# Norms of three groups summed over the partitions on GpSimd, row sums in fours, and equal last columns

## The chip, the cores and the metric

The kernel runs on one core of a Trainium2 chip. The metric is the time of one execution on the device, in microseconds. The engines are named as in the profile: PE is TensorE (PEld its weight loads), DVE is VectorE, ACT is ScalarE, POOL is GpSimd, and SP issues the DMAs.

## What is computed

Two layers of a decoder trunk over 1024 tokens of 1024 features, all in float32. In each layer one input projection feeds four mixers of 256 features each, called a, b, c and d; each group is normalized by itself, then all go through one output projection; a SwiGLU feed-forward block follows. Cut to what matters:

```python
for l in range(DEPTH):
    h = rmsnorm(x, attn_norm[l])
    proj = h @ w_in[l]
    y_a = mla_attention(...)        # latent attention, 4 heads, causal
    y_b = short_gated_conv(...)
    y_c = multiscale_pool(...)
    y_d = swa_sink_attention(...)   # window of 128 keys, a sink per head
    groups = jnp.stack([y_a, y_b, y_c, y_d], axis=2)
    gf = groups * lax.rsqrt(jnp.mean(groups * groups, axis=-1, keepdims=True) + RMS_EPS)
    x = x + (gf.reshape(b, s, D_MIX) * mix_norm[l]) @ w_o[l]
    h2 = rmsnorm(x, ffn_norm[l])
    gate, up = jnp.split(h2 @ w_gate_up[l], 2, axis=-1)
    x = x + (jax.nn.silu(gate) * up) @ w_down[l]
return rmsnorm(x, final_norm)
```

## The kernel before

Features lie on the 128 partitions and tokens along the free axis, so an activation of 128 features is a tile of 128 x 1024, kept as two halves `t` of 512 tokens. SBUF is managed as 47 slots (`u0` to `u46`) of two such halves. Every matrix product is made of three products of a rounded high part and a low part of each operand (`mm3`, L273), which `split` (L284, L285) makes with a cast on ACT and a subtraction on DVE.

*Norms.* `SumSq` squares tiles on ACT (L314, L319) and adds them on DVE (L324, L328), which leaves one tile of sums per partition. `rnorm` must then add over the partitions and give every partition the result: a product with a 128 x 128 matrix of ones on PE (L336) into a bank of PSUM. ACT takes logarithm, exponential and square (L338 to L340), DVE refines the root (L341, L344). `group_scale` does this for groups b, c and d in two halves, and multiplies the group by the result; `group_split` splits it for the output projection, whose products (`out_part`) read group d, then c, then b. Group a has its own `norm_a`.

*Window attention* (`swa_unit`). One unit is one block of 128 queries and one pair of heads: scores (L559) into PSUM, a masked minimum of negated scores (L569), two exponentials with row sums (L582), then on tiles of two columns the sink's term (L592, L593), its sum (L594), a reciprocal (L595), and the scaling (L597), transposes (L608) and products with the values (L620). Two units share the bank of the values, and what follows it.

*Latent attention* (`scores`, `mix_values`). For a head and a half, four blocks of 128 queries each get scores (L954 to L956), a maximum (L959, L962), exponentials with row sums (L973, L976), a sum of the two chunks' row sums where there are two (L985), a reciprocal (L986) and a scaling (L989, L992). `mix_values` transposes them (L1008), splits, and multiplies with the values (L1020). It works one step behind `scores`. In the last block POOL zeroes a part of the padded tile (L1017).

*Feed-forward.* The first of the 22 blocks of features is computed plainly for both halves, the others by a Strassen-like scheme (`gu_start` and after it, with L1234 copying a bank of PSUM to SBUF). For the plain block `plain_gates` multiplies the gate by the norm, `plain_silus` applies silu (L1368) and the norm again (L1369), and `plain_acts` multiplies by the other half of the block. The program calls them for the first half before the second half's norm, `norm(1)`, is taken. Silu belongs to another function table of ACT than logarithm and exponential.

*The end.* The last term of the last layer's down projection (`tail`, with `LAST_COLS`) is computed for four output tiles in two ranges of columns, so that the final norm and the output of the first range run beside the products of the second.

*Order.* The program is first written down in the order of the Python code. `order_engines` then arranges the instructions of each engine: `arrange` walks through a small model of the engines with a duration for each operation (`MM_NS`, `length`) and picks by rank, and the table `MOVED` shifts the rank of single steps. So the order on each engine comes from these numbers and not from the source alone.

Of the kernel before, what the change touches and what calls it, by code (L numbers as in the profile page):

```python
# [12 lines left out]
F32 = mybir.dt.float32  # L13
F32R = mybir.dt.float32r
AF = mybir.ActivationFunctionType
ALU = mybir.AluOpType
# [29 lines left out]
LAST_COLS = (slice(0, 384), slice(384, HT))  # L46
# [3 lines left out]
PC_N = 39  # L50
# [65 lines left out]
def trunk_kernel(ctx: ExitStack, tc: tile.TileContext, ins, out):  # L116
# [23 lines left out]
    nsink = cpool.tile([P, L * 4], F32, name="nsink")  # L140
# [158 lines left out]
    class SumSq:  # L299


        def __init__(self, n, direct=()):
            self.n, self.direct = n, direct
            self.acc = [None, None]
            self.done, self.rest = {}, {}
# [24 lines left out]
        def rnorm(self, t, cols=whole, tag="t"):  # L330

            a, n = F.ap(self.acc[t])[:, cols], self.n
            p = ps(tag)[:, cols]
            parts = [a] + [q for k, q in self.rest.items() if k == (t, cols.start)]
            for i, q in enumerate(parts):
                pe.matmul(p, ones, q, start=i == 0, stop=i == len(parts) - 1)  # L336
# [7 lines left out]
            dve.scalar_tensor_tensor(out=a, in0=q, scalar=1.5, in1=r0, op0=ALU.add, op1=ALU.mult)  # L344
            return self.acc[t]
# [83 lines left out]
    for l in range(L):  # L429
# [55 lines left out]
        if l == 0:  # L485
# [12 lines left out]
            for i in range(L):  # L498
                for o, c, n in ((nsink, PC_SINK, 4), (nffn, PC_FFN, NK)):
# [46 lines left out]
        psy_of = {}  # L546

        def swa_unit(g, i):
# [17 lines left out]
            nm, rs = small(2), small(2)  # L566
            for h in range(2):
# [6 lines left out]
                    scalar=nsink[:, l * 4 + 2 * g + h : l * 4 + 2 * g + h + 1],  # L574
# [4 lines left out]
            pr = tmp("tp")  # L579
            p3 = pr.rearrange("p (h k) -> p h k", h=2)  # L580
# [9 lines left out]
            es = small(2)  # L590
            sk = par[:, l * PC_N + PC_SINK + 2 * g : l * PC_N + PC_SINK + 2 * g + 2]
            dve.tensor_tensor(out=es, in0=nm, in1=sk, op=ALU.add)  # L592
            act.activation(es, es, AF.Exp)  # L593
            dve.tensor_tensor(out=rs, in0=rs, in1=es, op=ALU.add)  # L594
            dve.reciprocal(rs, rs)  # L595
# [16 lines left out]
            if i % 2 == 0:  # L612
                psy_of[g] = ps("pv")
            py = psy_of[g]
# [15 lines left out]
            if i % 2:  # L630
                pyv = py.rearrange("p (i h q) -> p i h q", i=2, h=2)
                tt = tmp("tn")
                tvs = [tt[rows, 0:256].rearrange("p (i q) -> p i q", i=2) for rows in (hd, tl)]
                for h, tv in enumerate(tvs):
                    act.copy(tv, pyv[tl, :, h, :])
                for h, (rows, tv) in enumerate(zip((hd, tl), tvs)):
                    o = F.ap(y["d"][g][t])[rows, (b - 1) * P : (b + 1) * P]
                    dve.tensor_tensor(
                        out=o.rearrange("p (i q) -> p i q", i=2),
                        in0=pyv[hd, :, h, :],  # L640
                        in1=tv,
                        op=ALU.add,
                    )

        units = deque((g, i) for g in range(2) for i in range(NK))

        def swa_some(n):
            for _ in range(n):
                if units and qs[2 * units[0][0]][1] is not None:
                    g, i = units.popleft()  # L650
                    swa_unit(g, i)
                    if i == NK - 1:
# [7 lines left out]
        def group_scale(g):  # L660

            sg = SumSq(2 * P)
# [267 lines left out]
        def scores(h, t, q):  # L930
# [3 lines left out]
            diag = ((own[0], 0), (own[1], 0), (own[0], P), (own[2], 0))  # L934
            for b in range(4):
# [9 lines left out]
                rs = small(2)  # L945
# [26 lines left out]
                if nch == 2:  # L972
                    act.activation(  # L973
                        chunks[0], pts[0], AF.Exp, bias=nm, scale=1.0, accum_out=rs[:, 1:2]
                    )
# [6 lines left out]
                    accum_out=rs[:, 0:1],  # L982
# [1467 lines left out]
```

## Time and profile before

| what | value |
|---|---|
| median of 3 runs | 2061.03 us (2056.88 to 2061.2) |
| profiled execution | 2059.23 us |
| its span, first to last instruction | 2057.4 us |
| granted clock of TensorE | 0.998 |
| PE busy | 2041.4 us (99%) |
| DVE busy | 1605.9 us (78%) |
| ACT busy | 988.1 us (48%) |
| POOL busy | 6.2 us |
| attention of layer 0, of layer 1 | about 103 to 390 us, 1045 to 1400 us |

Busy time is the union of an engine's instructions. Matmuls overlap in the pipeline, so what one costs is read from the start of one to the start of the next and not from its own duration (0.39 us for 512 columns). In a row of the groups of instructions stand line, engine, operation, tiles and shapes, count, then busy time, mean duration in ns, and the idle time before them with what ended it. In a row of the timeline stand start, duration, engine, line, operation and count, and in brackets the idle time before it. In a row of the waits stand who waited for whom, the sum in us, how often, and the longest.

### The profile page before, as it was taken

The numbers are of one execution on the slowest core, as the hardware profiler recorded it, in microseconds if no ns is written. First come the engines' busy times: TensorE is split into PE (matmuls) and PEld (weight loads), VectorE is DVE, ScalarE is ACT, GpSimd is POOL, SyncE is SP. The second block draws the span as 40 slices with busy tenths as digits, with TensorE's granted clock in tenths as the row PEclk, the third lists the DMA queues.
The fourth block names the chain that finished last, engine by engine and source line by source line (L and its number), as shares of the span: only waits on it lengthen the run. The fifth ranks groups of instructions, "written<-read, shape, count | busy, mean of one in ns | idle before, by whom it ended". The sixth has DMA issues, their size and how long they took to land.

```text
span 2057.4 us, 26139 instructions
## 1 busy us (share of the span) xinstructions
PE 2041.4 (99%) x9418; PEld 1681.8 (82%) x9418; DVE 1605.9 (78%) x2860; ACT 988.1 (48%) x1729; POOL 6.2 (0%) x36
## 2 busy tenths in 40 slices
PE   9999999999999999999999999999999999999998
PEld 7887888888888888888788878887888888888888
DVE  7889988999778778455576898989987877875555
ACT  6447666753333335344443666758433332354342
POOL 0000000000000000000000000000000000000000
PEclk9999999999999999999999999999999999999999
DMA  5020223255445448665401103142554544486642
GB/s 182 24 72 21 81 67 129 106 182 190 159 165 187 155 144 267 213 235 191 163 26 44 46 24 97 52 154 83 192 202 143 200 149 164 143 297 230 219 154 82
DMA packets 149233, 289.74 MB, mean 141 GB/s; under 512 B 12656, under 2 KB 72048, under 8 KB 149104
## 3 DMA queue, kind: packets, MB, share of 16 engines
q1 hardware_dynamic: 149104, 288.08, 41.7%
q8 instruction: 74, 1.21, 0.2%
q14 instruction: 55, 0.45, 0.1%
HBM read 204.66 MB, written 83.36 MB: 140 GB/s over the span
## 4 chain that ended last, share of the span: by engine, by line
PE 88%; DVE 6%; DMA 3%; ACT 2%; issue 1%; SPq 0%; DVEq 0%; ACTq 0%
PE ps_mm L273 35%; PE ps_s L273 26%; PE ps_t L273 9%; PE ps_pv L273 7%; PE ps_pv L1020 2%; DVE u L285 1%; PE ps_t L1008 1%; PE ps_t L336 1%; PE ps_s L954 1%; PE ps_s L956 1%; PE ps_s L955 1%; PE ps_s L559 1%; ACT u L284 1%; PE ps_pv L620 1%; PE ps_mm L819 1%
## 5 line engine op out<-in xcount | busy, mean ns | idle before, releaser
L273 PE MATMUL ps_mm<-u,u 128*128 128x512 f32 (+2 forms) x3376 | 878.7, 389 | 1.1 <-ACT u L287 0.6
L273 PEld LDWEIGHTS ps_mm<-u,u 128*128 128x128 f32 x3376 | 620.4, 188 | 130.6 <-issue 5.2
L273 PE MATMUL ps_s<-u,u 128*128 128x512 f32 x2666 | 694.9, 390 | 3.7 <-ACT tn L1234 2.0
L273 PEld LDWEIGHTS ps_s<-u,u 128*128 128x128 f32 x2666 | 499.3, 188 | 111.4 <-ACT tn L1234 3.6
L284 ACT CAST u<-u 128x1024 fp32r<-128x1024 f32 (+2 forms) x382 | 333.3, 893 | 462.1 <-DMA u<-ad 104.3
L285 DVE TENSOR_TENSOR u<-u,u 128x1024 fp32r<-128x1024 f32 (+2 forms) x382 | 385.8, 1025 | 165.6 <-ACT u L284 137.9
L273 PE MATMUL ps_t<-u,u 128*128 128x512 f32 (+2 forms) x1122 | 291.4, 382 | 0.5 <-ACT u L284 0.4
L273 PEld LDWEIGHTS ps_t<-u,u 128*128 128x128 f32 x1122 | 204.9, 188 | 43.0 <-issue 2.2
L273 PE MATMUL ps_pv<-u,u 128*128 128x512 f32 x744 | 204.6, 390 | 0.0
L273 PEld LDWEIGHTS ps_pv<-u,u 128*128 128x128 f32 x744 | 139.4, 188 | 29.6 <-ACT tn L1234 0.7
L1368 ACT ACTIVATE tp<-tp 128x512 f32<-128x512 f32 x88 | 55.5, 632 | 95.8 <-DVE tp L348 95.7
L287 ACT ACTIVATE u<-u,par 128x512 fp32r<-128x512 f32 x100 | 70.3, 719 | 43.3 <-DVE u L1157 16.5
L162 DVE TENSOR_TENSOR u<-u 128x256 f32<-128x256 f32 x176 | 73.5, 420 | 13.3 <-DMA u<-in_w_dn 11.0
L284 ACT CAST u<-ps_t 128x512 fp32r<-128x512 f32 (+3 forms) x128 | 61.0, 501 | 46.9 <-PE ps_t L1008 27.3
L285 DVE TENSOR_TENSOR u<-ps_t,u 128x512 fp32r<-128x512 f32 (+3 forms) x128 | 71.1, 576 | 12.8 <-ACT u L284 11.7
L288 DVE SCALAR_TENSOR_TENSOR u<-u,par,u 128x512 fp32r<-128x512 f32 x100 | 73.0, 746 | 3.3 <-ACT u L287 2.9
L319 ACT ACTIVATE tn<-u 128x512 f32<-128x512 f32 (+2 forms) x93 | 52.7, 592 | 37.1 <-DVE u L1619 29.2
L216 ACT CAST u<-u 128x1024 fp32r<-128x1024 f32 (+1 forms) x43 | 41.6, 970 | 57.6 <-DMA u<-in_w_in 27.5
L1369 DVE TENSOR_TENSOR tp<-tp,u 128x512 f32<-128x512 f32 x88 | 60.2, 685 | 10.4 <-ACT tp L1368 10.2
L1234 ACT COPY tn<-ps_s 128x512 f32<-128x512 f32 x64 | 37.3, 583 | 62.1 <-PE ps_s L273 62.1
L217 DVE TENSOR_TENSOR u<-u,u 128x1024 fp32r<-128x1024 f32 (+1 forms) x43 | 48.1, 1120 | 23.4 <-ACT u L216 9.7
L348 DVE TENSOR_TENSOR tp<-tp,u 128x512 f32<-128x512 f32 x84 | 57.3, 685 | 0.6
(192 smaller groups left out, 2028.4 us busy)
## 6 DMA issues: line engine op xcount, KB each, us to landing
u<-in_w_gu SPq DMA_DIRECT2D x88, 512.0 KB, 3.9
ad<-u SPq DMA_DIRECT2D x154, 256.0 KB, 2.5
u<-ad SPq DMA_DIRECT2D x70, 512.0 KB, 4.9
u<-in_w_dn SPq DMA_DIRECT2D x68, 512.0 KB, 4.0
qd<-u SPq DMA_DIRECT2D x44, 512.0 KB, 3.1
u<-qd SPq DMA_DIRECT2D x32, 512.0 KB, 5.0
u<-in_w_in SPq DMA_DIRECT2D x27, 512.0 KB, 3.5
u<-in_xT SPq DMA_DIRECT2D x32, 256.0 KB, 4.7
```

Of the source, the lines that this page charges most:

```text
L162: dve.tensor_tensor(out=o, in0=o, in1=u, op=ALU.add)
L216: act.copy(hi[:, :n], raw[:, :n])
L217: dve.tensor_tensor(out=lo[:, :n], in0=raw[:, :n], in1=rd(hi[:, :n]), op=ALU.subtract)
L273: pe.matmul(o, w, r, start=start and k == 0 and i == 0, stop=stop and k == n - 1 and i == 2, skip_group_check=again,)
L284: act.copy(hi, f)
L285: dve.tensor_tensor(out=lo, in0=f, in1=rd(hi), op=ALU.subtract)
L287: act.activation(hi, f, AF.Copy, scale=gain)
L288: dve.scalar_tensor_tensor(out=lo, in0=f, scalar=gain, in1=rd(hi), op0=ALU.mult, op1=ALU.subtract)
L319: act.activation(q, f, AF.Square)
L348: dve.tensor_tensor(out=o, in0=a, in1=b, op=ALU.mult)
L1368: last_silu = act.activation(g, g, AF.Silu)
L1369: dve.tensor_tensor(out=g, in0=g, in1=r, op=ALU.mult)
```

## The change

Five parts, and a new table of shifts, so that the order differs on every engine.

1. `SumSq` gets a flag `pool`. With it, `rnorm` sums over the partitions with one POOL instruction into half a slot of SBUF, and ACT and DVE read the sum there. `group_scale` sets it, so groups b, c and d use it: two halves each, in two layers. The other norms keep the product with ones.
2. Window attention works in pairs of blocks: scores and exponentials of both, then the sink's term, the sum and the reciprocal once on four columns, then the values of both. The sinks are laid out twice for that (8 columns per layer in place of 4).
3. Latent attention collects the row sums of four blocks in one tile and does the sum and the reciprocal once, behind the fourth; the scalings follow.
4. The plain gate keeps gate and up, each multiplied by the norm, in SBUF; all silus come after the second half's norm.
5. `LAST_COLS` becomes 256 and 256 columns in place of 384 and 128.

```diff
-LAST_COLS = (slice(0, 384), slice(384, HT))
+LAST_COLS = (slice(0, 256), slice(256, HT))
...
+            if self.pool:
+                s = F.half()
+                p = F.ap(s)
+                pool.partition_all_reduce(p, a, P, bass_isa.ReduceOp.add)
+            else:
+                p = ps(tag)[:, cols]
+                parts = [a] + [q for k, q in self.rest.items() if k == (t, cols.start)]
+                for i, q in enumerate(parts):
+                    pe.matmul(p, ones, q, start=i == 0, stop=i == len(parts) - 1)
...
-            sg = SumSq(2 * P)
+            sg = SumSq(2 * P, pool=True)
...
+            nm, rs, es = small(4), small(4), small(4)
+            p3 = [tmp("tp").rearrange("p (h k) -> p h k", h=2) for _ in range(2)]
+            for n in range(2):
+                hs = slice(2 * n, 2 * n + 2)
+                swa_scores(g, i + n, p3[n], nm[:, hs], rs[:, hs])
+            c = l * PC_N + PC_SINK + 4 * g
+            dve.tensor_tensor(out=es, in0=nm, in1=par[:, c : c + 4], op=ALU.add)
+            act.activation(es, es, AF.Exp)
+            dve.tensor_tensor(out=rs, in0=rs, in1=es, op=ALU.add)
+            dve.reciprocal(rs, rs)
...
-                if nch == 2:
-                    dve.tensor_tensor(out=rs[:, 0:1], in0=rs[:, 0:1], in1=rs[:, 1:2], op=ALU.add)
-                dve.reciprocal(rs[:, 0:1], rs[:, 0:1])
...
+            if t:
+                dve.tensor_tensor(out=rs[:, :4], in0=rs[:, :4], in1=rs[:, 4:], op=ALU.add)
+            dve.reciprocal(rs[:, :4], rs[:, :4])
...
-                gate = tmp("tp")
-                mul_to(gate, pg, r2[u])
-                raw_gates.append((f, u, gate, pu))
+                i, k = F.half(), F.half()
+                mul_to(F.ap(i), pg, r2[u])
+                mul_to(F.ap(k), pu, r2[u])
+                acts[f].append(i)
+                gates.append((i, k))
...
+            for i, k in gates:
+                a = F.ap(i)
+                last_silu = act.activation(a, a, AF.Silu)
+                mul_to(a, a, F.ap(k))
+                F.free(k)
...
-        plain_silus()
         combine(2)
         norm(1)
-        plain_acts()
...
         wn = GateUp(2)
-        plain_silus()
+        plain_acts()
...
-MM_NS = {512: 226.7, 384: 173.3, 256: 120.0, 128: 57.0}
+MM_NS = {512: 226.7, 384: 173.3, 256: 120.0, 128: 110.0}
...
+    if kind == "InstPartitionAllReduce":
+        return 3300
...
 MOVED = """
-0:-81.5 1:-224.5 2:-839.5 6:-142.5 9:-5 10:-375.5 11:-64 12:-2 13:-417.5 14:-44.5 15:4.5 17:-27 18:3 19:1.5
```

Three places show what that makes of the order. First POOL, from the start of the kernel to the second memset of latent attention in layer 0. Before:

```order
L2444 UNCONDITIONAL_BRANCH
L1017 MEMSET u20_2396 128x128 x2
L1017 MEMSET u26_2607 128x128 x2
L1017 MEMSET u17_2794 128x128 x2
L1017 MEMSET u19_3168 128x128 x2
```

In the change (an ISA row with two tiles is a sum over all partitions, in order for groups c, d and b; the one without tiles has no operands in SBUF):

```order
L2520 UNCONDITIONAL_BRANCH
L336 ISA
L336 ISA u8_1561<-u8_1561 128x512
L336 ISA u3_1576<-u3_1576 128x512
L336 ISA u4_1842<-u4_1842 128x512
L336 ISA u37_1857<-u37_1857 128x512
L1035 MEMSET u20_2319 128x128 x2
L336 ISA u45_492<-u15_1984 128x512
L336 ISA u45_492<-u46_493 128x512
L1035 MEMSET u17_2703 128x128 x2
```

Four sums now stand ahead of the first memset and two between the first and the second.

Next ACT in layer 0 at the first norm of group b, from the square of its second tile (L319) to the square of the root. Before, the logarithm L338 reads the bank `ps_t_2229`, which PE fills:

```order
L319 ACTIVATE tn_2226<-u37_2040 128x512
L314 ACTIVATE u45_492<-u30_711 128x512
L882 CAST u0_2177<-ps_mm_2178 128x4x64 x2
L338 ACTIVATE tn_2231<-ps_t_2229 128x512
L216 CAST vhi_2271<-vraw_2269 128x256
L339 ACTIVATE tn_2231<-tn_2231 128x512
```

In the change the logarithm is L343 and reads POOL's tile `u45_492`:

```order
L319 ACTIVATE tn_2160<-u37_1980 128x512
L995 ACTIVATE u15_1984,sm8_1985<-ps_s_2008,sm1_2007 128x512
L216 CAST vhi_2203<-vraw_2201 128x256
L216 CAST u2_2077<-u30_2075 128x768
L901 CAST u10_2123<-ps_mm_2124 128x4x64
L284 CAST u34_2102<-te_2100 128x512
L901 CAST u10_2123<-ps_mm_2124 128x4x64
L343 ACTIVATE tn_2164<-u45_492 128x512
L344 ACTIVATE tn_2164<-tn_2164 128x512
L345 ACTIVATE tn_2165<-tn_2164 128x512
L319 ACTIVATE tn_2174<-u37_1980 128x512
L284 CAST u19_2304<-ps_t_2300 128x384
```

Six rows of other work stand between square and logarithm where three stood, and behind the three steps of the root come the square of the other half and the casts of transposed probabilities (`u19_2304` and on).

Last ACT at the start of layer 0's feed-forward, around the second half's norm. Before, silu (L1368) with its table stands ahead of that norm (`tn_4205`), and the copy of PE's bank behind it:

```order
L284 CAST u15_4213<-u40_4007 128x1024
L1368 ACT_TABLE_LOAD
L1368 ACTIVATE tp_4121<-tp_4121 128x512
L284 CAST u29_4192<-tp_4183 128x512
L338 ACT_TABLE_LOAD
L338 ACTIVATE tn_4205<-ps_pv_4203 128x512
L284 CAST u16_4189<-tp_4184 128x512
L339 ACT_TABLE_LOAD
L339 ACTIVATE tn_4205<-tn_4205 128x512
L340 ACTIVATE tn_4206<-tn_4205 128x512
L1234 COPY tn_4276<-ps_s_4262 128x512
```

In the change:

```order
L343 ACTIVATE tn_4083<-ps_pv_4081 128x512
L284 CAST u28_4067<-tp_4062 128x512
L344 ACTIVATE tn_4083<-tn_4083 128x512
L345 ACTIVATE tn_4084<-tn_4083 128x512
L284 CAST u31_4074<-tp_4063 128x512
L1136 ACTIVATE te_4094<-u21_3325,par_75 128x512
L1137 ACTIVATE te_4095<-u32_2351,par_75 128x512
L1252 COPY tn_4154<-ps_s_4140 128x512
```

The first copy (L1234, now L1252) stands behind a norm without a table load; one load and two silus follow seven rows further on.

More of the change, by code (lines that the diff above doesn't have):

```diff
@@ L589, in swa_unit, with swa_values @@
                 )
[L590 to L595, printed above, removed]
+        def swa_values(g, i, p3, rs, py):
+            nkb = 2 if i else 1
+            c0 = 0 if i else P
             for h in range(2):
@@ L629, in swa_unit @@
             R.free(tlo)
[L630 to L643, printed above, removed]
@@ L647, in swa_some @@
+        units = deque((g, i) for g in range(2) for i in range(0, NK, 2))
+        due = [0]
         def swa_some(n):
-            for _ in range(n):
+            due[0] += n
+            while due[0] > 1:
+                due[0] -= 2
                 if units and qs[2 * units[0][0]][1] is not None:
                     g, i = units.popleft()
-                    swa_unit(g, i)
-                    if i == NK - 1:
+                    swa_units(g, i)
+                    if i == NK - 2:
                         for h in range(2):
@@ L1756 @@
 DRAM_TILES = {"xs", "xp", "xr", "qd", "out"} | {f"ad{n}" for n in range(7)}
-BUFS = {"ps_mm": 2, "ps_s": 3, "ps_t": 2, "ps_pv": 1, "te": 2, "tn": 3, "tp": 3, "vraw": 2, "vhi": 2, "vlo": 2, "sm1": 16, "sm2": 16, "sm16": 2}
+BUFS = {"ps_mm": 2, "ps_s": 3, "ps_t": 2, "ps_pv": 1, "te": 2, "tn": 3, "tp": 3, "vraw": 2, "vhi": 2, "vlo": 2, "sm1": 16, "sm4": 16, "sm8": 16, "sm16": 2}
 def in_psum(a):
```

81 lines of the change are left out of this document (40 added, 41 removed), and 616 rows, old and new, of the table MOVED.

## Prediction

> **What bounds the kernel now.** I read the page first, then the waits of TensorE, then busy times by stage, then the timeline at the places that the change touches. The page says that TensorE (PE) is busy for 99% of the span and carries 88% of the chain that ended last:
>
> ```profile
> span 2057.4 us, 26139 instructions
> PE 2041.4 (99%) x9418; PEld 1681.8 (82%) x9418; DVE 1605.9 (78%) x2860; ACT 988.1 (48%) x1729; POOL 6.2 (0%) x36
> PE 88%; DVE 6%; DMA 3%; ACT 2%; issue 1%; SPq 0%; DVEq 0%; ACTq 0%
> ```
>
> Of 2057.4 us PE is idle for 16, and half of that is the drain after its last product. The longest entry of PE's own waits is:
>
> ```profile
> PE ps_s L273 <- ACT tn L1234: 2.0, 2, 1.0
> ```
>
> So time is won almost only by taking work from PE, and lost by making it wait. The stages in which PE could be made to wait are the four stretches of attention, where VectorE (DVE) is nearly as full as PE. The columns are the stretch, its length, then the busy time of PE, of weight loads, of DVE, of ACT and of POOL:
>
> ```profile
> 103.00:210.00 107.00, 107.00 (x503) 86.12 (x502) 96.37 (x210) 67.29 (x142) 0.00 (x0) 1.00 0.14 45
> 210.00:390.00 180.00, 179.91 (x901) 148.13 (x900) 160.57 (x363) 118.85 (x261) 3.09 (x16) 1.00 0.31 103
> 1045.00:1225.00 180.00, 180.00 (x868) 147.41 (x867) 140.34 (x323) 91.91 (x211) 0.00 (x0) 1.00 0.12 37
> 1225.00:1400.00 175.00, 174.25 (x872) 142.05 (x872) 154.61 (x353) 110.95 (x247) 2.95 (x16) 1.00 0.31 102
> ```
>
> In layer 0's attention (103 to 390 us) DVE works 257 of 287 us, in layer 1's (1045 to 1400) 295 of 355. POOL does nothing there but 3 us of memsets.
>
> **1. Twelve products with ones leave PE.** The norms of groups b, c and d are two per group and layer, 3 x 2 x 2 = 12. One of them in the timeline, with what follows it:
>
> ```profile
> 220.09 1.02 PE L336 MATMUL ps_t<-u,ones 128*128 128x512 f32 x2
> 220.54 1.03 PE L273 MATMUL ps_s<-u,vhi 128*128 128x512 f32 x2
> 221.41 0.40 PE L273 MATMUL ps_s<-u,vlo 128*128 128x512 f32 x1
> ```
>
> The plain product that starts at 220.54 seems to follow after 0.45 us, but its successor comes only at 220.54 + 1.03 - 0.39 = 221.18, and the third at 221.41, 0.23 later. From 220.09 to 221.41 stand this fp32 product and two plain ones of 0.23, so the fp32 product costs 1.32 - 0.46 = 0.86 us of PE. Nothing hides it, since PE is never idle there: 12 x 0.86 = **10.3 us less**.
>
> **2. The last columns are cut 256 + 256 in place of 384 + 128.** Four outputs, 11 blocks and 3 products make 132 products at each width. Their pitch is read from start to start:
>
> ```profile
> 2021.38 11.60 PE L273 MATMUL ps_mm<-u,u 128*128 128x384 f32 x66
> 2032.82 2.79 PE L273 MATMUL ps_t<-u,u 128*128 128x128 f32 x24
> 2035.45 0.86 PE L336 MATMUL ps_s<-u,ones 128*128 128x384 f32 x2
> 222.47 0.52 PE L273 MATMUL ps_mm<-vhi,u 128*128 128x256 f32 x3
> 222.82 0.28 PE L273 MATMUL ps_mm<-vlo,u 128*128 128x256 f32 x1
> ```
>
> 384 columns take 11.44 / 66 = 0.173 us, 128 take 2.63 / 24 = 0.110, not a third of that, and 256 take 0.35 / 3 = 0.117 (0.120 by (0.52 - 0.28) / 2). Per pair of products 0.283 becomes 0.234 to 0.240: 132 x 0.043 to 0.049 = 5.7 to 6.5, I take **6.0 us less**.
>
> **3. The drain behind the last product gets longer**, because all of it now has 256 columns. Rows at 384 and at 128 columns bracket it:
>
> ```profile
> 2033.02 0.56 DVE L1619 TENSOR_TENSOR u<-u,ps_mm 128x384 f32<-128x384 f32 x1 [2.05 <-PE ps_mm L273]
> 2036.99 0.49 ACT L338 ACTIVATE tn<-ps_s 128x384 f32<-128x384 f32 x1 [2.86 <-PE ps_s L336]
> 2049.00 0.29 DVE L1619 TENSOR_TENSOR u<-u,ps_mm 128x128 f32<-128x128 f32 x1 [2.86 <-PE ps_mm L273]
> 2049.54 0.49 PE L336 MATMUL ps_s<-u,ones 128*128 128x128 f32 x2 [0.58 <-DVE u L324]
> 2050.29 0.28 ACT L338 ACTIVATE tn<-ps_s 128x128 f32<-128x128 f32 x1 [0.66 <-PE ps_s L336]
> 2052.01 2.19 DVE L418 SCALAR_TENSOR_TENSOR u<-u,par,u 128x128 f32<-128x128 f32 x8
> L418 DVE SCALAR_TENSOR_TENSOR u<-u,par,u 128x384 f32<-128x384 f32 x8 | 4.5, 610 | 0.0
> L418 DVE SCALAR_TENSOR_TENSOR u<-u,par,u 128x128 f32<-128x128 f32 x8 | 2.2, 347 | 0.0
> ```
>
> Half of each difference is added: three DVE steps (the sum, two of the norm) 3 x 0.13, four ACT steps 4 x 0.105, from the products with ones to the logarithm 1.54 at 384 and 0.75 at 128, so 0.40 more, and eight scalings 8 x 0.13 = 1.05. That is 2.3. The last output transfers double in size; no row isolates that, I take 0.3 (0 to 1). **2.6 us more.**
>
> **4. Two table loads of ACT per layer go.** Now the first half's silu stands ahead of the second half's norm, so ACT's function table is loaded three times more around it, and the copy that frees PE's bank comes late:
>
> ```profile
> 408.52 1.28 ACT L338 ACT_TABLE_LOAD   x1
> 410.94 1.28 ACT L339 ACT_TABLE_LOAD   x1
> 413.44 0.57 ACT L1234 COPY tn<-ps_s 128x512 f32<-128x512 f32 x1
> 414.06 2.11 PE L273 MATMUL ps_s<-u,u 128*128 128x512 f32 x8 [0.96 <-ACT tn L1234]
> ```
>
> With all silus behind both norms the copy stands ahead of the one load that is left. The 2.57 us of loads cover the wait of 0.96 and its twin in layer 1, which together are the 2.0 of the waits. What is late next there is DVE, so I take the 2.0 and no more: **2.0 us less** (0 to 2.6). The rewritten gate has as many DVE passes as before.
>
> **5. Twelve sums on POOL are added.** No row shows this operation. One DVE pass over two such tiles is its floor; seven halvings of 128 partitions with one such pass each is a tree; 127 passes one by one is the far end:
>
> ```profile
> L348 DVE TENSOR_TENSOR u<-u,u 128x512 f32<-128x512 f32 x39 | 25.8, 682 | 0.1
> ```
>
> That is 0.7 us, 4.8 us and 87 us. I take 3 us, by the tree, since one instruction is to do the whole sum; the ends stay for the rivals. By time alone it is nothing (12 x 3 = 36 us on an empty engine). What counts is who waits: ACT's logarithm now waits for POOL, and behind it on ACT stand the casts of transposed probabilities that PE multiplies next. The order of the change puts six ACT rows between the square and that logarithm for one half of group b, one of them with a read of its accumulator. By rows of now:
>
> ```profile
> L976 ACT ACTIVATE u<-ps_s,sm 128x512 f32<-128x512 f32 x16 | 11.0, 690 | 4.0 <-DVE sm L986 2.8 <-DVE sm L962 1.2
> L976 ACT ACTIVATION_READ_ACCUMULATOR u<-ps_s,sm 128x1 f32 x64 | 12.9, 201 | 0.0
> L216 ACT CAST u<-u 128x768 fp32r<-128x768 f32 x16 | 13.4, 839 | 7.7 <-DMA u<-in_w_o 6.6 <-PE ps_t L1008 1.0
> L216 ACT CAST vhi<-vraw 128x256 fp32r<-128x256 f32 x18 | 7.3, 406 | 13.6 <-PE ps_mm L273 6.5 <-DMA vraw<-in_w_uq 4.2 <-PE ps_s L273 2.9
> L882 ACT CAST u<-ps_mm 128x256 fp32r<-128x256 f32 x16 | 5.4, 379 | 1.0 <-DVE u L217 0.6 <-PE ps_mm L273 0.4
> 222.56 0.62 ACT L284 CAST u<-te 128x512 fp32r<-128x512 f32 x1
> ```
>
> 0.69 + 0.20 + 0.41 + 0.84 + 2 x 0.38 + 0.62 = 3.5 us; the DVE add ahead of the sum takes 0.7 of it, so a sum of up to about 2.8 us holds nobody. At 3 us it holds ACT for 0.2, twelve times: **2 us more** (0 if PE has other work, 24 at the tree's 4.8 us with nothing to hide it). POOL's memsets in the padded probabilities queue behind the sums, and PE waits for those too. The first two of now:
>
> ```profile
> 213.40 0.35 POOL L1017 MEMSET u<- 128x128 f32 x2 [212.97 <-PE ps_mm L273]
> 250.60 0.34 POOL L1017 MEMSET u<- 128x128 f32 x2 [36.85 <-PE ps_s L956]
> ```
>
> In the change the two sums of group b stand between them, and 37 us have room for twice 3 us: nothing, up to sums of about 15 us.
>
> **6. Row sums in fours** (two blocks of the window, four of the latent attention) remove small DVE steps:
>
> ```profile
> L986 DVE RECIPROCAL sm<-sm 128x1 f32<-128x1 f32 x64 | 9.6, 156 | 0.8 <-ACT u L976 0.3
> L595 DVE RECIPROCAL sm<-sm 128x2 f32<-128x2 f32 x32 | 5.0, 160 | 0.2
> ```
>
> 48 reciprocals of the first kind, 16 of the second, and by the same 0.16 us 24 + 32 adds: 120 steps, about 19 us of DVE over both layers. None of it is PE's time; it offsets what step 5 takes from DVE. The scalings start only behind the fourth block, but their transposes belong to the next step of the loop, so a step's whole PE work covers that. I take 0 (a gain of 2 to a loss of 2). The parameters' load grows from 86 to 94 columns and moves up by one place on SP, ahead of the first input block: nothing either, by half a us at the start at most.
>
> **Sum**: -10.3 - 6.0 + 2.6 - 2.0 + 2 = -13.7 us. The profiled execution took 2059.2, of which 1.8 lie around the span; 2045.5. The median of the runs shown is 1.8 above it, so I predict **2047 us**, 2043 to 2051 by steps 2 to 6 alone.
>
> **Rivals.** *The sum outlasts its cover* (slower). Place: ACT's logarithm, its casts behind it, PE behind those. Every us beyond 2.8 is 12 us; without step 5's 2 us the gain is 15.7, so it decides at 2.8 + 1.3 = 4.1 us. At 6 us it is 12 x 3.2 = 38 more: 2061 - 16 + 38 = 2083; at the far end of 87 us 12 x 84 more, 3053. For it: the tree's price of 4.8; against: PE's queue holds products that need no ACT, and the reads of b stand last in each output product. Chance 0.11, 0.03 of it for sums of tens of us. [...]
>
> *DVE becomes the bound* (smaller gain). For 36 us POOL reads beside a DVE that is 90% busy in layer 0. If DVE stood still all that time, its load there would be 257 - 9.5 + 18 = 266 us against PE's 287 - 5 = 282: still below, but at 94% the waits in between reach PE. Priced at a sixth of 36 us, 6 us: 2053, up to 2059. For it: the four stretches; against: the 19 us that step 6 gives back. Chance 0.16. [...]
>
> *The new order closes other waits too* (larger gain). Of PE's 16 us of idle time about 7 are the drain and 2 are step 4's; with the other 7 gone and step 5 at nothing it is 2047 - 9 = 2038. Chance 0.10: order and buffers change everywhere, but most of these waits are the start and bank turns that the change does not touch.
>
> *The products were filled time* (no change): PE's freed time is waited away on the same DVE chain. PE's zero idle in the first and third stretch speaks against it. 2059 to 2063, chance 0.03.
>
> **How the numbers follow.** Forecast 0.60, rivals 0.11, 0.16, 0.10, 0.03. 0.2% is 4.1 us, about what a measurement of this kernel tells from no change. Faster: 0.60 + 0.10 + 0.11 of the second rival = 0.81; same: 0.03 + its other 0.05 = 0.08; slower 0.11. The range 2037 to 2057 leaves out the slower rival, the last one, and the far tail of the second.
>
> **What would show it.** Right: L336's products fall from 33 to 21 calls, PE busy near 2025, the tail's 132 pairs 6 us shorter, no wait on the copy at 414, POOL's twelve sums near 3 us each with ACT's wait on them under 0.5. Wrong: sums above 4 us with PE waiting on casts behind a logarithm; two-input DVE passes longer than 0.68 us beside a sum; a drain longer than 11 us after the last product.

## The result, and the profile after

The changed kernel takes 2076.3 us (median of four runs, 2076.04 to 2076.46), the kernel before 2059.7 beside it: 1.0082 of it, interval 1.0070 to 1.0094. It is 16.6 us slower, where 14 us less were forecast. The page of the changed kernel begins:

```profile
span 2074.7 us, 26000 instructions
PE 2036.9 (98%) x9394; PEld 1670.6 (81%) x9394; DVE 1609.2 (78%) x2740; ACT 980.2 (47%) x1707; POOL 48.9 (2%) x48
```

Before, PE was idle for 16 us of the span; now it is for 37.8. Its busy time fell by 4.5 us only, though some 16 us of products are gone. Busy time is a union and hides slow products, so I added up, over all products, by how much each start lies behind the usual distance for its width in the traces (0.227 us behind 512 columns, 0.120 behind 256, and so on): 36 us before, 68 now, give or take 3 us by which of the smallest lags are counted. These some 30 us more, less 10.3 us of products with ones (the prediction's price) and 5.3 of last products, with 1.6 more of drain, come near the 17.3 us by which the span grew. PE's waits, in us, how often, the longest:

```profile
PE ps_mm L273 <- DVE te L355: 6.9, 4, 3.9
PE ps_t L1026 <- DVE u L285: 3.0, 3, 2.0
PE ps_mm L273 <- DVE u L903: 3.0, 3, 1.7
PE ps_t L273 <- DVE u L1632: 2.4, 2, 1.9
PE ps_s L273 <- ACT tn L1252: 1.5, 1, 1.5
```

Where the longest entry was 2.0 us behind ACT, PE now waits mostly for DVE. By stage (length, then busy time of PE, weight loads, DVE, ACT, POOL, and the granted clock):

```profile
103.00:210.00 107.00, 102.07 (x485) 82.69 (x483) 94.65 (x188) 63.15 (x130) 14.04 (x4) 1.00 0.12 40
210.00:390.00 180.00, 175.94 (x861) 142.48 (x862) 156.79 (x320) 113.12 (x251) 9.77 (x18) 0.98 0.29 97
390.00:445.00 55.00, 55.00 (x240) 44.43 (x239) 54.99 (x87) 39.13 (x63) 0.00 (x0) 1.00 0.30 105
445.00:775.00 330.00, 326.19 (x1430) 267.31 (x1429) 264.66 (x418) 114.15 (x157) 0.00 (x0) 1.00 0.52 173
1045.00:1225.00 180.00, 178.94 (x865) 147.27 (x864) 131.95 (x288) 88.22 (x197) 7.92 (x3) 1.00 0.11 36
1225.00:1400.00 175.00, 166.95 (x832) 133.70 (x831) 149.31 (x307) 105.83 (x240) 16.97 (x20) 1.00 0.24 78
```

Of the four stretches with sums (POOL's busy time shows them) three lose 4 to 7 us of PE's busy time, and the one from 1045 us loses 1. But 445 to 775 us, in the feed-forward part, where no sum runs, loses 4 too. Before, PE was never idle there:

```profile
445.00:775.00 330.00, 330.00 (x1457) 272.76 (x1456) 268.26 (x420) 115.49 (x159) 0.00 (x0) 1.00 0.50 169
```

The 390 to 445 row is the place of the plain gate: PE's wait there is gone, as step 4 said.

The sums themselves, and the group of two-tile passes of DVE that scale groups by their norm among others (busy, mean ns):

```profile
L336 POOL PARTITION_ALL_REDUCE u<-u x12 | 42.0, 3501 | 1085.2 <-DVE u L324 1073.6 <-DVE sm L1006 7.4 <-DMA vraw<-in_w_uq 4.2
L355 DVE TENSOR_TENSOR u<-u,u 128x512 f32<-128x512 f32 x44 | 38.3, 893 | 0.1
```

A sum takes 3.5 us, near the 3 assumed. The passes take 0.89 us in the mean in place of 0.68. Why, and what comes of it, the timeline shows at the longest wait:

```profile
205.44 0.68 DVE L349 SCALAR_TENSOR_TENSOR u<-tn 128x512 f32<-128x512 f32 x1
205.61 3.60 POOL L336 PARTITION_ALL_REDUCE u<-u  x1 [3.69 <-DVE u L324]
206.37 3.01 DVE L355 TENSOR_TENSOR u<-u,u 128x512 f32<-128x512 f32 x2
209.30 0.68 DVE L355 TENSOR_TENSOR te<-ps_mm,u 128x512 f32<-128x512 f32 x1
210.03 2.35 PE L273 MATMUL ps_mm<-u,u 128*128 128x512 f32 x4 [3.88 <-DVE te L355]
```

The two scalings of the first half take 3.01 us in place of 1.29 while the sum of the second half runs. Behind them on DVE stands the pass that frees the bank PE wants, and PE waits 3.88 us for it. The granted clock (the last column but two) then reads:

```profile
209.50:216.30 6.80, 6.27 (x14) 4.59 (x15) 6.80 (x12) 4.47 (x8) 0.00 (x0) 0.50 0.01 2
216.30:223.00 6.70, 6.70 (x30) 5.50 (x30) 4.75 (x8) 2.54 (x8) 0.35 (x2) 1.00 0.00 0
```

After the wait PE runs at half clock up to 216.3 us, busy for 6.27 us, half of which, about 3 us, is lost.

### The profile page after: what moved, and what is told of

Its sections match the earlier page's. It is cut to its first block, busy times and chain, and to the rows that moved or that the text cites. A ratio compares the mean times of both kernels' runs of the same rounds, so it can differ in the third digit from the quotient of the medians.

```text
span 2074.7 us, 26000 instructions
## 1 busy us (share of the span) xinstructions
PE 2036.9 (98%) x9394; PEld 1670.6 (81%) x9394; DVE 1609.2 (78%) x2740; ACT 980.2 (47%) x1707; POOL 48.9 (2%) x48
## 5 line engine op out<-in xcount | busy, mean ns | idle before, releaser
L273 PE MATMUL ps_mm<-u,u 128*128 128x512 f32 (+1 forms) x3376 | 872.6, 390 | 10.6 <-DVE te L355 6.9
L273 PE MATMUL ps_s<-u,u 128*128 128x512 f32 x2666 | 686.9, 391 | 4.5 <-ACT tn L1252 1.5
L284 ACT CAST u<-u 128x1024 fp32r<-128x1024 f32 (+2 forms) x382 | 333.4, 893 | 459.7 <-DMA u<-ad 84.5
L273 PE MATMUL ps_t<-u,u 128*128 128x512 f32 (+1 forms) x1122 | 284.1, 378 | 2.4 <-DVE u L1632 2.4
L273 PE MATMUL ps_pv<-u,u 128*128 128x512 f32 x744 | 197.2, 390 | 1.2 <-DVE u L285 1.2
L284 ACT CAST u<-ps_t 128x512 fp32r<-128x512 f32 (+3 forms) x128 | 61.5, 501 | 63.5 <-PE ps_t L1026 29.7
L1252 ACT COPY tn<-ps_s 128x512 f32<-128x512 f32 x64 | 37.4, 584 | 78.6 <-PE ps_s L273 67.6
L319 ACT ACTIVATE tn<-u 128x512 f32<-128x512 f32 (+1 forms) x93 | 53.0, 592 | 32.9 <-DVE u L1632 25.1
L336 POOL PARTITION_ALL_REDUCE u<-u x12 | 42.0, 3501 | 1085.2 <-DVE u L324 1073.6
```

The costliest lines, as they stand in the source:

```text
L273: pe.matmul(o, w, r, start=start and k == 0 and i == 0, stop=stop and k == n - 1 and i == 2, skip_group_check=again,)
L284: act.copy(hi, f)
L319: act.activation(q, f, AF.Square)
L336: pool.partition_all_reduce(p, a, P, bass_isa.ReduceOp.add)
```

## The experiments

Three theories. **A, the hold** (in the expectations and in e14's name: the port): a sum holds DVE's passes over two SBUF tiles, as the 3.01 us above suggest, and PE waits for what is queued behind them; what inside the chip would hold them no run shows. **B, the late answer**: a sum answers about 2.5 us later than a product with ones (3.50 us in the mean against 1.02 at 220.09 us in before), and what stands behind the logarithm on ACT and DVE comes late with it. **C, the order**: the new table of shifts puts instructions so that PE waits more, whatever the sums do. All runs, beside 2059 to 2061 us of the kernel before:

| run | what it is | us | ratio, interval |
|---|---|---|---|
| e1_products | change, products with ones | 2082.3 | 1.0109, 1.0095 to 1.0123 |
| e2_sums | before, sums | 2115.5 | 1.0272, 1.0258 to 1.0286 |
| e3_columns | before, columns 256 + 256 | 2056.0 | 0.9983, 0.9974 to 0.9992 |
| e4_unread | e1, unread sums beside | 2103.1 | 1.0214, 1.0200 to 1.0228 |
| e5_beside | before, unread sums, order kept | 2075.9 | 1.0073, 1.0057 to 1.0089 |
| e6_late | before, late logarithms, order kept | 2088.8 | 1.0132, 1.0117 to 1.0148 |
| e7_both | before, both, order kept | 2089.3 | 1.0138, 1.0121 to 1.0155 |
| e8_sums_fit | change, table searched freely | 2126.5 | 1.0322, 1.0308 to 1.0336 |
| e9_products_fit | e1, table searched freely | 2116.5 | 1.0274, 1.0254 to 1.0293 |
| e10_hold | change, two-tile passes kept off sums | 2084.1 | 1.0117, 1.0102 to 1.0133 |
| e11_hold_fit | e10, attention searched narrowly | 2080.2 | 1.0092, 1.0078 to 1.0107 |
| e12_products_fit | e1, attention searched narrowly | 2065.8 | 1.0026, 1.0017 to 1.0035 |
| e13_columns_fit | e3, attention searched narrowly | 2062.0 | 1.0014, 1.0005 to 1.0023 |
| e14_no_port | change, order kept, late answer without a sum | 2073.0 | 1.0067, 1.0054 to 1.0079 |
| e15_at_once | change, order kept, answer at once | 2067.2 | 1.0035, 1.0022 to 1.0047 |
| e16_gate_fit | e3 and the plain gate | 2059.1 | 0.9995, 0.9986 to 1.0004 |
| e17_columns_bare | e3 without any table | 2094.1 | 1.0163, 1.0143 to 1.0184 |
| e18_parts_bare | e1 without any table | 2087.6 | 1.0137, 1.0120 to 1.0155 |

### One part at a time

e1_products takes the flag back, e2_sums puts it and `rnorm`'s new branch into the kernel before, e3_columns changes one line of before, e4_unread has both product and sum:

```diff
-            sg = SumSq(2 * P, pool=True)
+            sg = SumSq(2 * P)
```

> The changed kernel with the twelve norms of groups b, c, d taken by products with ones again, all else as in the change. Theory A (POOL's sums hold DVE's passes over two SBUF tiles, and PE waits for what is queued behind them) and theory B (a sum answers 2.5 us later than a product, and ACT and DVE stand in order behind it) both say: PE gets 10.3 us of products back, the stalls of PE beside the sums, about 22 us, go: near 2076 + 10 - 22 = 2064, and stalls of PE near 205 and 1234 us are gone. Theory C (the loss comes from the other parts or from the new order): 2076 or more, up to 2087.

> The kernel before with the twelve sums on POOL alone. Theories A and B: 10.3 us of PE go, 22 us of stalls come, near 2060 + 12 = 2072, and each two-tile pass of DVE that meets a sum takes 1.4 to 2.4 us instead of 0.69. Theory C: the sums gain what the prediction said, near 2050.

```diff
-LAST_COLS = (slice(0, 384), slice(384, HT))
+LAST_COLS = (slice(0, 256), slice(256, HT))
```

> The kernel before with last columns of 256 and 256 alone. By the prediction's steps 2 and 3: 6.0 less of PE, 2.6 more of drain, near 2060 - 3.4 = 2056.5; the drain behind the last product 2.6 us longer. Theory C, if the columns are part of what costs: 2060 or more.

```diff
+                s, b = F.half(), F.half()
+                pool.partition_all_reduce(F.ap(s), a, P, bass_isa.ReduceOp.add)
```

> The changed kernel with products with ones for the twelve norms, and beside each of them the sum on POOL, whose result nobody reads; the norm goes to a tile of its own, so that it doesn't wait for the sum. Theory A: the sums hold DVE as before (13 us of DVE in all) although nobody waits for their results: 8 to 20 us slower than the kernel with products alone, 2073 to 2085. Theory B: within 2 us of the kernel with products alone, near 2065.

The columns gave 3.3 us where 3.4 were forecast. On the page of e3_columns PE is busy for 5.3 us less than before:

```profile
span 2053.3 us, 26140 instructions
PE 2036.1 (99%) x9418; PEld 1675.4 (82%) x9418; DVE 1606.4 (78%) x2860; ACT 987.5 (48%) x1729; POOL 6.3 (0%) x36
```

The drain, from the end of the last product of the down projection (2034.38 + 8.08, first row) to the span's end, is now 10.8 us. From the end of the last product with ones (2043.49 + 0.70) it is 9.1, where it was 7.1:

```profile
2034.38 8.08 PE L273 MATMUL ps_mm<-u,u 128*128 128x256 f32 x66
2043.49 0.70 PE L336 MATMUL ps_s<-tn,ones 128*128 128x256 f32 x2 [0.59 <-ACT tn L319]
```

In the kernel before, the drain from 2041.43 + 7.53 to 2057.4 was 8.4 us, so it grew by 2.4:

```profile
2041.43 7.53 PE L273 MATMUL ps_mm<-u,u 128*128 128x128 f32 x66
```

e1 was the surprise: with the sums gone the kernel became 6 us slower, 2082, and not 2064. Theory C had 2076 to 2087. But e4, with sums that nobody reads, is 21 us slower than e1, where A had 8 to 20 and B at most 2, and e2 is 56 us slower than before, far beyond A and B. In all these the planner also made another order for the other instructions, so they mix three causes. The next runs keep an order.

### Hold and late answer in the order of before

In e5_beside, e6_late and e7_both the rows on PE, DVE, ACT and SP stand as in the kernel before. POOL gets the extra work, and in the last two the logarithm takes its bias, a column of zeros, from what POOL writes:

```diff
+                # e5
+                pool.tensor_copy(extra[0][:, 0:1], a[:, 0:1])
+                pool.partition_all_reduce(extra[0], cst[:, CC_TRI : CC_TRI + HT], P, bass_isa.ReduceOp.add)
...
+                # e6
+                pool.tensor_copy(extra[0][:, 1:2], a[:, 0:1])
+                for i in range(20):
+                    k = P * (1 + i % 3)
+                    pool.memset(extra[0][:, k : k + P], 0.0)
+                pool.memset(extra[0][:, 0:1], 0.0)
...
+                # e7
+                pool.partition_all_reduce(extra[0], a, P, bass_isa.ReduceOp.add)
+                pool.memset(extra[0][:, 0:1], 0.0)
...
-            act.activation(r0, p, AF.Ln, scale=1.0 / n)
+            act.activation(r0, p, AF.Ln, bias=late, scale=1.0 / n)
```

> The kernel before with the order of every other engine kept word for word; beside each of the twelve products with ones POOL sums a constant tile of 128x512 into a scratch tile that nobody reads. It starts when the accumulator is ready, by a copy of one column, and nobody waits for it. So only what the sum takes from others is left. Theory A (port): two-tile passes of DVE that meet a sum take 1.4 to 2.4 us, 13 to 17 us of DVE in all, and the kernel is 10 to 25 us slower, 2070 to 2085. Theory B (latency): no more than 3 us slower. Theory C (order): the same.

> The kernel before, order kept; the products with ones stay, but the logarithm behind each of the twelve also waits for a chain of small memsets on POOL that starts when the accumulator is ready and takes about 3.6 us, as long as a sum, and reads no tile. So only the later answer is left, with the products' 10.3 us not saved. Theory A: two-tile passes of DVE stay at 0.69 us and the kernel is within 5 us of before. Theory B: 10 to 25 us slower. Theory C: the same as before.

> The kernel before, order kept; the products stay, and the logarithm behind each of the twelve also waits for a sum on POOL over the same accumulator (through a column that is set to zero behind it). So port and latency act together, and the 10.3 us of products aren't saved. If the two add up, it is as much slower as the last two together; less 10.3 us this is what the sums alone cost in an order made for products, to be set beside the 56 us of the kernel with sums alone, where the planner also changed the order. Theory A: near the kernel with sums beside. Theory B: near the kernel with late logarithms. Theory C: at most 10 us slower than before.

Both are real here: 15 us by the hold alone (e5), 28 by the late answer alone (e6). C, which allowed at most 3, 0 and 10 us, was wrong for this order. Together the two are 29 and not 43, presumably since a pass that is held while others wait for the sum anyway costs nothing more. Where a sum that nobody reads meets two scalings (e5):

```profile
204.71 3.23 POOL L341 PARTITION_ALL_REDUCE extra<-cst  x1
205.05 3.05 DVE L353 TENSOR_TENSOR u<-u,u 128x512 f32<-128x512 f32 x2
```

And how a late answer, with no sum at all, reaches PE (e6; the chain on POOL takes 3.1 to 3.8 us at eleven places, as a sum does, and 5.1 at this one, where its first copy takes 2.1): the last small memset releases the logarithm, whose root releases a DVE pass, behind which stands the last addition for the next norm, for which PE waits 3.24 us.

```profile
207.51 0.10 POOL L344 MEMSET extra<- 128x1 f32 x1
207.64 0.69 ACT L347 ACTIVATE tn<-ps_t,extra 128x512 f32<-128x512 f32 x1 [5.72 <-POOL extra L344]
209.68 0.69 DVE L350 SCALAR_TENSOR_TENSOR tn<-ps_t,tn 128x512 f32<-128x512 f32 x1 [3.73 <-ACT tn L349]
210.29 0.68 DVE L325 SCALAR_TENSOR_TENSOR u<-tn,u 128x512 f32<-128x512 f32 x1
211.03 1.93 PE L337 MATMUL ps_t<-u,ones 128*128 128x512 f32 x2 [3.24 <-DVE u L325]
```

### Other tables of shifts

e8_sums_fit and e9_products_fit keep the instructions of the change and of e1, and get a table searched over the whole program; e8's planner also has two-tile passes stand still until 2.5 us behind a sum's start, as long as the first scaling above was held (from 206.37 us it took 2.40, so without its usual 0.68 it stood until 208.09, 2.48 behind 205.61):

```diff
-                ns += 0.8 * sum(max(0.0, min(b, t + ns) - max(a, t)) for a, b in pool_busy[-8:])
+                d = t
+                for a, b in pool_busy[-8:] if v.two else ():
+                    if b - a > 1000 and a <= t + ns - 60:
+                        d = max(d, a + 2500)
+                ns += d - t
```

> The changed kernel with another table of shifts, searched for longer, and with the planner told what the traces show: a pass of DVE over two SBUF tiles stands still until 2.5 us after the start of a sum. All instructions are those of the change; only their order on the engines differs. Theory C (the sums are worth their 10.3 us, and the order that came with them loses it again): the stalls beside the sums shrink from 22 us to under 8 and those elsewhere from 10 to under 5, near 2076 - 20 = 2056 or less, down to 2046. Theories A and B (the sums cost more than they save wherever they stand): no better than 2070.

> The changed kernel with products with ones for the twelve norms, and a table of shifts searched for as long as the last one. Theory C: the 23 us that this kernel had over before with a table made for sums go, and with the columns' 3.3 and the gate's 2 it is near 2055; the kernel with sums and a fitted order is then up to 10 us faster than this one. Theories A and B: this one is the faster of the two by 8 us or more.

Both came out far above every time named: 2126 and 2116. C missed; A and B had said no better than 2070, and e9 the faster by 8 us or more, and it is, by 10. These orders have waits all over the feed-forward part. Presumably they fit the planner's durations to the last nanosecond, and the chip's differ; no run isolates that. So the same instructions cost 50 us (change) and 34 us (e1) more by their order alone, which is more than any part of this change.

e10_hold adds a rule to the planner, beside e8's duration, and e11 to e13 get shifts searched within attention only, with slack asked for (e13 also the planner's longer duration for 128 columns):

```diff
+        if v.two and wait is None:
+            for a, b in pool_busy[-8:]:
+                if b - a > 1000 and a - 600 <= t < a + 2400:
+                    wait = a + 2400
```

> The changed kernel with one rule more in its planner: while a sum runs, DVE takes the passes that read PSUM or one tile first, and a pass over two SBUF tiles waits until 2.4 us after the sum's start. The instructions are the same; only the order near the sums moves. Theory A (port): fewer stalls of PE beside the sums, 22 us to about 12, near 2066. Theory B (latency): the logarithm still comes 2.5 us later, so within 3 us of 2076.

> The last kernel with the shifts of steps inside attention (150 to 440 and 1180 to 1420 us) searched again, the feed-forward part left as it came, and a search that keeps slack: a shift counts only if it also helps when every answer comes 60 ns and every DMA 0.5 us later. Theory C (the order that came with the change loses what the sums gain): stalls beside the sums under 8 us, 2050 to 2060. Theories A and B (the sums cost as much as they save): no better than the products' kernel searched in the same way.

> The changed kernel with products with ones, and the shifts of steps inside attention searched in the same way. Theory C: stalls fall from 59 to about 45 us, near 2066, and the kernel with sums searched likewise is up to 10 us faster than this. Theories A and B: this one is as fast as that or faster, 2055 to 2068.

> The kernel before with columns of 256 and 256, the planner's duration of a product of 128 columns raised to what it takes, and the shifts of steps inside attention searched in the same way. PE waits for only some 10 us there, so all theories: 2050 to 2056, at best 6 us below the columns alone. If it is slower than the columns alone, such a search fits the planner and not the chip, and the last two runs say less.

e10 misses what A and B said, and refutes the simple form of A. The held passes get shorter, by their group's mean from 893 to 798 ns:

```profile
L355 DVE TENSOR_TENSOR u<-u,u 128x512 f32<-128x512 f32 x44 | 34.1, 798 | 0.3
```

Yet the kernel is 8 us slower than the change. Our reading is that a pass that waits in the order is as late as one that is held beside the sum. e12 shows what the order was worth with products: 16 us off e1, with the same instructions, by moving shifts in attention, to 2065.8. C had 2066, but A's and B's 2055 to 2068 fits as well. e11 did not follow: with sums the same search ends 14 us above e12, as A and B said and C did not. e13 warns about the search, which, with the longer duration, made the columns' kernel 6 us slower. So these runs show that order carries such amounts. In both pairs searched alike the kernel with sums is the slower one, by 10 and 14 us; what a sum costs in a good order they don't settle.

### Taking the sums apart in the change's own order

Here the change's rows on PE, DVE, ACT and SP are kept word for word, and only POOL's instruction differs:

```diff
-                pool.partition_all_reduce(p, a, P, bass_isa.ReduceOp.add)
+                pool.tensor_copy(p[:, 0:1], a[:, 0:1])
+                for i in range(20):    # 4 in e15_at_once
+                    pool.memset(p[:, i % 4 * P : i % 4 * P + P], 1.0)
```

> The changed kernel, its order on PE, DVE, ACT and SP kept row for row; each sum on POOL is replaced by a copy of one column of the accumulator and twenty small memsets of the tile that the sum would write, about 3.5 us in all, as long as a sum. The sum itself is left out (the tile holds ones). So the late answer stays and the reading of SBUF goes. Theory A (port): the 13 us of held passes go, and most of the 22 us of stalls beside the sums: 2058 to 2064. Theory B (late answer): 2073 to 2077.

> The same with four memsets in place of twenty, about 1 us: neither a late answer nor a held port is left, so this is the change with sums for nothing, in its own order. Theories A and B, if the sums alone make the loss: stalls as in before, 36 us, near 2060 - 10.3 - 3.3 - 2 = 2045. Theory C (the order and the other parts cost too): 10 us of stalls away from the sums remain, 2054 or more.

Without the hold 2073.0, 3.3 us less, as B said; with an answer at once as well 2067.2, another 5.8, which leaves what C said. Together the sums cost 9.1 us in their own order, nearly the 10.3 that their products were priced at. (e15's stand-in still takes 0.9 to 1.6 us.) At the place shown above the two scalings are back at 1.29 us (first row, e14), and PE's wait falls from 3.88 us by steps, to 2.14:

```profile
206.84 1.29 DVE L357 TENSOR_TENSOR u<-u,u 128x512 f32<-128x512 f32 x2
208.78 0.73 PE L273 MATMUL ps_mm<-u,u 128*128 128x512 f32 x2 [2.14 <-DVE te L357]
```

and in e15 to 1.67:

```profile
206.88 0.68 DVE L357 TENSOR_TENSOR te<-ps_mm,u 128x512 f32<-128x512 f32 x1
207.62 0.73 PE L273 MATMUL ps_mm<-u,u 128*128 128x512 f32 x2 [1.67 <-DVE te L357]
```

Even this wait has half a clock behind it (e15, the stretch from 208.4 us):

```profile
208.40:211.60 3.20, 2.85 (x7) 2.28 (x8) 3.20 (x6) 1.81 (x3) 0.00 (x0) 0.50 0.02 5
```

Those 1.67 us are no sum's: the pass that frees PE's bank simply stands behind two scalings in this order. The stages of e15 show losses without sums elsewhere too; PE is busy for 1.8, 3.2 and 3.7 us less than before in these:

```profile
210.00:390.00 180.00, 178.11 (x882) 144.69 (x882) 158.16 (x326) 115.75 (x254) 4.97 (x26) 1.00 0.31 102
445.00:775.00 330.00, 326.76 (x1435) 268.32 (x1434) 264.26 (x415) 114.46 (x157) 0.00 (x0) 1.00 0.51 169
1225.00:1400.00 175.00, 170.56 (x841) 136.09 (x842) 147.14 (x305) 107.64 (x243) 5.64 (x26) 1.00 0.28 93
```

The middle one shows the order alone. No instruction of the change runs there: between the seventh copy of PE's bank (L1234, in the change L1252) and the last but one in that layer, all 365 passes of DVE in the change are also among the 379 of before, but only 233 of them stand in a common order with those. e3_columns, which gained what was forecast, keeps all 379 in order.

With sums for nothing the change should have stood at 2060.3 - 10.3 - 3.3 = 2046.7, with the prediction's 10.3 for the products. It stands 20.5 us above. Either the order costs these, or one of the parts without sums does.

> The kernel before with the columns of 256 and 256 and the plain gate of the change, the shifts around that gate alone searched again, no sums and no row sums in fours. By the prediction's step 4 two waits of 1.0 us and two table loads per layer go: 2054, 2 below the columns alone. Theory C (each new order loses something): 2056 to 2062.

e16 is e3 with the gate part of the change's diff and new shifts around it. The gate gave nothing, as C said: 2059.1 against 2056.0 of the columns alone. PE's two waits of 1.0 us on the copy became one of 0.8, and two for DVE came:

```profile
PE ps_mm L273 <- DVE u L285: 2.4, 2, 1.4
PE ps_s L273 <- ACT tn L1234: 0.8, 1, 0.8
```

### The parts without any table

```diff
-MOVED = """
...
-"""
+MOVED = ""
```

> The kernel before with columns of 256 and 256 and the longer duration for products of 128 columns, with no table of shifts at all: the planner's plain order. If the order alone carries tens of microseconds (theory C), this is 20 to 50 us slower than the 2056 with the table. If the order matters little, 2056 to 2065.

> The changed kernel with products with ones, so pairs, row sums in fours and the plain gate are left of the change, also with no table of shifts. It differs from the last kernel in these three parts alone. If they cost nothing by themselves, it is within 8 us of that kernel; if one of them is what costs the 20 us that the stand-ins leave, it is 15 us slower or more.

In the planner's plain order the kernel with pairs, row sums in fours and the plain gate is 6.5 us faster than the one without them, not slower. DVE is busy for 7 us less; first e17_columns_bare:

```profile
PE 2054.7 (98%) x9418; PEld 1682.4 (80%) x9418; DVE 1614.9 (77%) x2860; ACT 988.6 (47%) x1729; POOL 6.9 (0%) x36
```

and e18_parts_bare:

```profile
PE 2048.9 (98%) x9418; PEld 1678.3 (80%) x9418; DVE 1607.6 (77%) x2740; ACT 978.8 (47%) x1707; POOL 5.8 (0%) x36
```

So these parts show no cost of 20 us by themselves. The two plain orders differ as well, so the 6.5 us are no measure of the parts alone. And the table of before takes 38 us out of its kernel (2094 to 2056, with the planner's one duration for 128 columns besides), while the table of the change, made with sums, takes 5 out of the change with products (2088 to 2082). That is theory C, in part shown and in part by exclusion. Shown is that order alone moves the same instructions by 16 us (e1 to e12), and that it costs 3.2 us in one stretch without any instruction of the change. That all of the missing 20 us are the worse order is inferred. It stays open whether an order as good as that of before exists for these instructions: the best one found, e12, is still 10 us above the columns alone. The version that beats both kernels is e3_columns, the columns alone.

## Why the prediction was wrong

**The step that failed is the sum**: "The profiled execution took 2059.2", and from it only what the parts take and add. That charged nothing for the order being made anew on every engine. The 16 us of PE's idle time were taken as a floor, and the only rival that spoke of the order ("The new order closes other waits too") let it move one way. By e15 the kernel misses 20.5 us with sums for nothing, the largest term of all, and by e12, e17 and e18 it is put down to the new order; a loss by the order had no chance in the prediction. With the sums' 9.1 us it leads from 2046.7 to the 2076.3 measured. The row that could have warned was the first one: PE busy for 99%, in attention beside a DVE at 90%, rests on an order fitted to its own instructions, as e17 shows, and an edit after which the planner orders anew gives that up.

**Step 1** stands by its count: the group of these products has 52 records before and 28 after, two to a product. Its price of 0.86 us was not measured by itself; PE is busy for 9.1 us less in the change than in e1, which has the twelve products back in another order.

**Steps 2 and 3** were right: 3.3 us measured, 3.4 forecast, with both terms a little smaller. The products gave 5.3 of 6.0 us. The drain behind the last product of the down projection grew by 2.4 us with the columns alone and by 1.9 in the change; 2.6 was forecast.

**Step 4** named the wait rightly, and it went. The gain of 2.0 us did not come: in e16 other waits took its place, among them 2.4 us for DVE, which the step had named as what is late next.

**Step 5** had the sum's length (3.5 us against 3), by luck, since its 3 was a choice between 0.7 and 87 us and its own tree gave 4.8. It mis-sized the price: 9.1 us in place of 2, 5.8 by the late answer and 3.3 by the hold. It looked for the harm on ACT, behind the logarithm. It came on DVE, which carries the next passes of the same chain and, behind them, those that free PE's banks. In the change PE's waits on ACT's casts (L284) come to about 2 us, those on DVE to about 22. In the order of before the same late answer costs 28 us, so a cover counted in one order says little about another.

**Step 6** is not contradicted: with the row sums in fours e18 is not slower than e17, though they were never run alone in a fitted order. DVE gained less than counted: its busy time falls by 7 us from e17 to e18, not by 19.

Of the rivals, *the sum outlasts its cover* was to decide at 4.1 us, and did harm at 3.5. *DVE becomes the bound* named the hold, with two-tile passes as the sign to look for. That DVE would stand still was its supposition, and a sixth of the sums' 36 us, its price of 6 us, a choice; the hold cost 3.3. The trace shows the first scaling held, 2.40 us from 206.37 in place of 0.68, but not for the whole sum as recorded: the second, also over two SBUF tiles, took 0.68 us from 208.69, while the sum's record, if it can be trusted that far, ends at 209.21.

## What to carry to other kernels

When an edit makes a planner order a full kernel anew, price the order as a term of its own, with a loss as well as a gain; what is at stake is what the kernel loses without its table (here 38 us), and an experiment that keeps the order row for row tells it from the rest. Work moved to an idle engine is not free when its answer comes later (here 5.8 us in the change's own order and 28 in that of before): ask which passes stand behind the waiting one on each engine in between, and not only on the next. Take the independent small gain alone first; here the equal columns, which kept the order, are worth more without the rest.

## What the hardware showed

**Half clock behind a wait.** Behind some of PE's waits the granted clock fell to 0.50: for 6.8 us behind one of 3.88 (the change, from 209.5 us), for at least the 3.2 us shown behind one of 1.67 (e15, from 208.4). Not every wait near 2 us did it: behind those of 1.72 us at 229.5 and of 2.03 at 1252.4 in the change the clock stayed at 1.00. What tells these apart no run shows. With the about 3 us lost at half clock the wait of 3.88 us cost about 7.

**The sum over all partitions** took 3.2 to 3.9 us for 128x512 in float32 in the change, where the prediction took 3. ACT's passes showed no delay beside it: squares of 128x512 in SBUF (L314) took 0.63 us at 165.91 and 167.03 with a sum running, and 0.63 at 188.05 without.
